# Idle transposes ahead of a kernel's first products, two pool groups in one PSUM tile, and a tail whose order is written out by hand

## The chip, the core and the metric

The kernel runs on one core of a Trainium2 chip. The metric is the device time of one launch in microseconds (us), lower is better. The runs of the kernel before shown here are three, with a median of 2133.31 us (2133.0 to 2134.68); one further execution was profiled, and every view below is of that one.

## What is computed

One layer of a streaming encoder on 256 tokens of width 2048, all in float32. Cut to what matters:

```python
x = x + 0.5 * swiglu(rms_norm(x, ffn1_norm), w_gate, w_up, w_down)        # first FFN, 5632 wide
h = rms_norm(x, mix_norm)
u, q, k, v, g, a_lr = jnp.split(h @ w_in, IN_SPLITS, axis=-1)
y_pool = pool_mixer(u, pool_w, pool_scale)     # 4 groups of 256 channels: trailing mean minus token, @ pool_w[g], * scale
y_gla  = gla_mixer(q, k, v, g, a_lr, ...)      # 4 heads of gated linear attention in chunks of 64, per-head norm, gate
x = x + concat(y_pool, y_gla) @ w_out
x = x + mem_cross_attention(rms_norm(x, xattn_norm), rms_norm(mem, mem_norm), w_q, w_kv, w_o)
x = x + 0.5 * swiglu(rms_norm(x, ffn2_norm), w_gate, w_up, w_down)        # second FFN
return rms_norm(x, final_norm)
```

Weights come from memory once, as float32. Nearly all the work is matrix products of 256 tokens with weights.

## The kernel before, in words

**Split products.** Each float32 operand is written as a rounded high part and a remainder, both of type fp32r: a product is then three matmuls, (high, high), (high, low) and (low, high). Weights arrive in `raw` tiles of 128x2048; ACT casts them to `wh` (line 228) and DVE subtracts to get `wl` (line 229). `in_turn` keeps these splits in their order on each of the two engines. Activations are split the same way into `xs` and `ys`: `split_scaled` does the high part on ACT (line 210) and the remainder on DVE (line 211).

**The stream.** Class `Stream` holds a list of items: units (a load of 1 MB of weights, with the matmuls that use it) and operations between them. `st.op(f, n)` places f behind the n-th unit that follows. `emit` walks the list, splits weights up to two units ahead (one ahead for the first four units) and loads three units ahead, on the queue of SP. So the code has an order, but the order of instructions on each engine is made by the planner (`schedule_with_timeline_sim=True`, line 1291): it runs through the program in a simulated time of its own and places what is ready. Two calls bind it: `issue_after(ins)` keeps instructions behind `ins` on that engine, and `keep_in_program_order` keeps one behind all that stands before it in the code on its engine. Once made, the order is fixed: an engine that waits for one instruction holds all behind it.

**PSUM.** All of PSUM is one pool of four tiles, each 128x2x512 float32 (`ptile`; a half of 512 columns is a bank). A tile is free again when its last reader is done.

**Start (lines 531 to 585, 719 to 724).** `gain_columns` clears a 128x128 tile on DVE and then loads the first norm's 16 rows of weights into it on the queue of ACT; `turn_gains` (539, 540) transposes it on TensorE and copies the columns to `gains`. `x_chunk(c)` transposes the c-th 256 columns of x by four transposes (line 575) and splits them scaled by `gains`; unit c of the first block reads what chunk c makes. Chunk c stands ahead of unit c-1. `x_squares` makes the sums for the norm on ACT (line 244). x chunks and the first weights are loaded in turn on the queue of SP.

**Feed-forward.** `block_t` is an ordinary block: eight units of 24 matmuls of 128x512. `block_s` uses Strassen-like sums for the unit pairs 0, 2 and 4: `part_sums` (lines 346 to 356, through `pair_sums`) makes sums of activations on DVE in a tile `T`, `add_weights` (363 to 367) sums of weights in the same one-buffer tile `T`, and `seven` (401) does seven products.

**Mixer.** `pool_unit` (line 805) does the per-group maps of the pool: for each of four groups g a PSUM tile of its own, with 256 columns of each bank used; `pool_out` scales and splits the result (210, 211) into `ys`. It stands between the block of k, whose evictions use line 266, and the blocks of v. For each GLA head, `scores` makes the scaled copies of q on ACT and DVE (line 933), the score matmuls (941) and the copies to the single tile `ST` (947); `attend` multiplies with v (954, 957) and evicts (963, 965); `head_squares`, `head_norms` (976; 186 reads its PSUM tile) and `head_scale` (207, 990) do the per-head norm. Heads 0 and 1 follow the first block of v, heads 2 and 3 the second; in both, scores stand 1 + i units behind their block, attend 2 + i. Then the two gate blocks (line 292, evicted through lines 265, 266 and 268) follow.

**Tail (lines 1157 to 1231).** The last product is split in token halves h: for each column block nb (four of 512) and half, `end_evict` adds to x on DVE (1188), squares and sums on ACT (1191), and multiplies by the final norm's weights on GpSimd (1193; all but the last block of the second half). `row_factor(h)` makes the factor per token (1196, 186 to 198) and `finish` scales a block (ACT 1207, DVE 1209, or 1203 with both factors) and stores it from the queue of SP (1210): four stores of 256 KB per half. Nothing fixes the order of DVE and ACT here but the planner.

Of the kernel before, what the change touches and what calls it, by code (L numbers as in the profile page):

```python
# [20 lines left out]
NB = 512  # L21
# [4 lines left out]
EPS = 1e-6  # L26
# [4 lines left out]
G_FFN1, G_MIX, G_X, G_MEM, G_FFN2, G_PS, G_HN, G_BA, G_END = 0, 16, 32, 48, 64, 80, 88, 96, 100  # L31
# [61 lines left out]
def build(ctx, tc, I, out):  # L93
    nc = tc.nc
# [22 lines left out]
    def ptile(name):  # L117
        return psum.tile([P, 2, NB], F32, tag="ps", name=name)
# [6 lines left out]
    def uid(s):  # L125
        cnt[0] += 1
        return f"{s}{cnt[0]}"
# [45 lines left out]
    def gcol(i):  # L173
        return gains[:, i : i + 1]
# [3 lines left out]

    def f32(ap):
        return ap.bitcast(F32)  # L180


    def rsqrt(dst, sums, n, w):
# [25 lines left out]
    def split_scaled(dst, kt, src, scale):  # L209
        hi = nc.scalar.activation(dst[:, kt, 0, :], src, AF.Copy, scale=scale)  # L210
        nc.vector.scalar_tensor_tensor(  # L211
            out=dst[:, kt, 1, :], in0=src, scalar=scale, in1=f32(dst[:, kt, 0, :]),
            op0=ALU.mult, op1=ALU.subtract,
        )
        return hi
# [314 lines left out]

    def gain_columns(names, queue):
        t = rows["gain"] = scope["pool"].tile([P, P], F32, tag="gain", name=uid("gain"), bufs=2)
        nc.vector.memset(t, 0.0)
        for name, at, n in names:
            queue.dma_start(t[at : at + n, :], I[name].rearrange("o (k p) -> (o k) p", p=P))

    def turn_gains(lo, hi):
        ps = ptile(uid("pgain"))
        nc.tensor.transpose(ps[:, 0, :P], rows["gain"], ident)
        nc.vector.tensor_copy(gains[:, lo:hi], ps[:, 0, lo:hi])  # L540

    xrows = {}

# [21 lines left out]
    def x_cols(c, n):  # L565

        b = c // (2 * NB)
        return xrows[b][:, :, c - b * 2 * NB : c - b * 2 * NB + n]

    def x_chunk(c):  # L570
        v = ptile(uid("px"))[:, 0, :].rearrange("p (a b) -> p a b", a=2)
        k = 2 * c
        for j in range(2):
            for h in range(2):
                nc.tensor.transpose(  # L575
                    v[:, j, h * P : (h + 1) * P], x_cols((k + j) * P, P)[:, h], ident
                )
        for j in range(2):
            rows["hi", c] = split_scaled(xs, k + j, v[:, j, :], gcol(G_FFN1 + k + j))
# [64 lines left out]

    PAIRS = (0, 2, 4)

    def pair_sums(g, delay):
        def f():
            if g == PAIRS[0]:
# [12 lines left out]
    def ffn(wg, wu, wd, down):  # L662
# [33 lines left out]
        for lo, n in FF_PARTS:  # L696
# [19 lines left out]
                st.op(lambda n=n: turn(gate[0], 4 * (n - 1)), 1)  # L716
            down(wd, 4 * lo, 4 * n, lo + n == FF // NB)

    st.op(lambda: turn_gains(0, G_MIX))
    for c in range(8):  # L720
        st.op(lambda c=c: x_chunk(c), c - 1)
    for c in range(8):
        st.op(lambda c=c: x_squares(c), 6)
    st.op(lambda: finish_norm(8, False), 7)
# [3 lines left out]
    def down_first(wd, k0, nk, last):  # L728
        into_x(wd, ys, 0.5, G_MIX if last else None, k0, nk, src=None if k0 else I["x"][0])

    for g in PAIRS:
        pair_sums(g, 5)
    ffn(I["ffn1_w_gate"][0], I["ffn1_w_up"][0], I["ffn1_w_down"][0], down_first)
    st.op(close_scope, 1)
    st.op(open_scope("s_mix"), 1)
# [62 lines left out]
    def pool_unit(wh, wl):  # L798
        wh, wl = (w.rearrange("p (g t d) -> p g t d", g=4, t=2) for w in (wh, wl))
        for g in range(4):  # L800
            ps = ptile(uid("pp"))
            for dt in range(2):
                parts = [(w, ct, a) for ct in range(2) for w, a in ((wh, 0), (wl, 0), (wh, 1))]
                for n, (w, ct, a) in enumerate(parts):
                    nc.tensor.matmul(
                        ps[:, dt, :S], w[:, g, ct, dt * P : (dt + 1) * P],
                        ys[:, 8 + 2 * g + ct, a, :], start=n == 0, stop=n == 5,
                    )
            mix["pp", g] = ps

    def pool_out(g):
        for dt in range(2):
            split_scaled(ys, 2 * g + dt, mix["pp", g][:, dt, :S], gcol(G_PS + 2 * g + dt))

    def load_a(raw):
        nc.sync.dma_start(
# [189 lines left out]
    for b in range(2):  # L1006
        block_b(wblock(w_in, (4 + b) * NB), xs, ev_v(b))
        for i in range(2):
            h = 2 * b + i
            st.op(lambda h=h: scores(h), 1 + i)  # L1010
            st.op(lambda h=h: attend(h), 2 + i)
            st.op(lambda h=h: head_squares(h), 2 + i)
        st.op(lambda b=b: head_norms(b), 4)
        st.op(lambda b=b: head_scale(b), 5)
    block_a(wblock(w_in, 6 * NB), xs, ev_g(0))
# [137 lines left out]
    def down_end(wd, k0, nk):  # L1153

        acc_ps, kept = {}, []

        def mm(b, k, h, wh, wl):

            wh, wl = (w.rearrange("p (k j n) -> p k j n", j=2, n=NB) for w in (wh, wl))
            for j in range(2):  # L1160
                nb = 2 * b + j
                if nb not in acc_ps:
                    acc_ps[nb] = ptile(uid("pe"))
                for kk in range(2):
                    products(acc_ps[nb][:, h, :], ys, k + kk, h, wh[:, kk, j], wl[:, kk, j],
                             k + kk == 0, k + kk == nk - 1)
                if k == nk - 2:
                    end_evict(nb, h)
# [12 lines left out]

        def end_evict(nb, h):
            cols = slice(nb * NB, (nb + 1) * NB)
# [3 lines left out]
            xn, o = x_cols(nb * NB, NB)[:, h], fin[nb][:, h]  # L1187
            nc.vector.scalar_tensor_tensor(
                out=xn, in0=acc_ps[nb][:, h, :], scalar=0.5, in1=xn, op0=ALU.mult, op1=ALU.add
            )  # L1190
            nc.scalar.activation(o, xn, AF.Square, accum_out=ss[:, h, nb : nb + 1])
            if nb < 3 or h == 0:
                nc.gpsimd.tensor_tensor(out=o, in0=xn, in1=fin["gB"][:, cols], op=ALU.mult)

        def row_factor(h):
            nc.vector.tensor_reduce(out=sums[:, h : h + 1], in_=ss[:, h, :4], axis=AX.X, op=ALU.add)
            rsqrt(Rcol[:, h : h + 1], sums[:, h : h + 1], D, 1)

        def finish(h, c, engine=None):
            cols = slice(c * NB, (c + 1) * NB)  # L1200
            x, o, r = fin[c][:, h], x_cols(c * NB, NB)[:, h], Rcol[:, h : h + 1]
            if h == 1 and c == 3:
                nc.vector.scalar_tensor_tensor(
                    out=o, in0=o, scalar=r, in1=fin["gB"][:, cols], op0=ALU.mult, op1=ALU.mult
                )
            elif engine is nc.scalar:
                nc.scalar.activation(o, x, AF.Copy, scale=r)
            else:
                nc.vector.tensor_scalar_mul(o, x, r)
            nc.sync.dma_start(out[0, h * P : (h + 1) * P, cols], o)  # L1210
# [12 lines left out]

        def ready_sqrt():
            tc.keep_in_program_order(nc.scalar.activation(sums, Rcol, AF.Sqrt))

        st.op(ready_sqrt, 8)
        st.op(last_gain, 2)
        for b in range(2):
            st.op(lambda b=b: fetch_x(b), 1 + 2 * b)  # L1230
        for b in range(2):
            for i, src in enumerate(wwide(wd, b * 2 * NB, k0, nk - 2)):
                st.unit(src, unit(b, 2 * i))
        for b in range(2):
            st.unit(wwide(wd, b * 2 * NB, k0 + nk - 2, 2)[0], end_unit(b))
        st.op(second_half)
# [73 lines left out]
```

## Time and profile before

| what | value |
|---|---|
| median of 3 runs | 2133.31 us |
| the profiled execution's own time | 2133.11 us |
| its span, first to last instruction | 2131.2 us |
| TensorE (PE) busy | 2111.3 us, 99% |
| weight loads (PEld) busy | 1768.5 us, 83% |
| DVE busy | 1427.7 us, 67% |
| ACT busy | 1008.0 us, 47% |
| DMA | 435.91 MB, mean 205 GB/s |

Times in the views count from the span's start. In a row of the timeline the first number is the start, the second how long the row lasts; "x4" says that it merges four instructions, and the bracket gives the engine's idle time before it and what ended that. Matmuls are pipelined: one row's length reaches into the next, so the distance from one start to the next is what a matmul costs. 1.9 us of the profiled execution's own time lie outside its span.

### The profile page before, as it was taken

To read this page: it belongs to the slowest core of one execution; us is meant where nothing else is said; L and a number is where in the kernel's file an instruction comes from. 1 tells how busy PE (TensorE), PEld (TensorE's weight loads), DVE (VectorE), ACT (ScalarE), POOL (GpSimd) and SP (SyncE) were. 2 spreads that over 40 slices of the span, in tenths; PEclk is the share of its full clock that TensorE was granted. 3 is DMA by queue.
4 is the path that set the end of the run, shared out by engine and by line. 5 is a ranking of instruction groups with operands and counts; after the bars stand their busy time and mean duration, and the time that the engine had idled before them with its cause. 6 is when DMAs were issued, how large, how long until landed. Compare 5 with 4: busy or idle time off the path is not lost.

```text
span 2131.2 us, 24070 instructions
## 1 busy us (share of the span) xinstructions
PE 2111.3 (99%) x10032; PEld 1768.5 (83%) x10032; DVE 1427.7 (67%) x1189; ACT 1008.0 (47%) x890; POOL 14.2 (1%) x41
## 2 busy tenths in 40 slices
PE   9999999999999999999999999999999999999998
PEld 7878888888888888888888888888888888888886
DVE  8876588856864576565666454567874888658744
ACT  7554354534534545455445443445443455434433
POOL 0000000000000000000000000000000000000001
PEclk9999999999999999999999999999999999999999
DMA  7556665566656655557654555666576665766663
GB/s 277 197 189 234 224 221 195 186 233 226 227 178 234 221 162 180 167 185 278 222 190 161 167 169 171 195 207 207 175 247 217 214 209 175 249 212 223 221 217 119
DMA packets 143316, 435.91 MB, mean 205 GB/s; under 512 B 9828, under 2 KB 13000, under 8 KB 142824
## 3 DMA queue, kind: packets, MB, share of 16 engines
q1 hardware_dynamic: 143176, 434.38, 60.5%
q8 instruction: 78, 1.28, 0.2%
q14 instruction: 30, 0.25, 0.0%
q10 hardware_dynamic: 32, 0.01, 0.0%
HBM read 417.58 MB, written 16.78 MB: 204 GB/s over the span
## 4 chain that ended last, share of the span: by engine, by line
PE 98%; DVE 1%; issue 0%; ACT 0%; DMA 0%; SPq 0%; DVEq 0%; ACTq 0%
PE pt L307 58%; PE pa L292 15%; PE pt L401 12%; PE pb L307 6%; PE pe L307 3%; PE ph L691 1%; PE pl L1084 1%; PE pv L1119 1%; PE px L621 0%; DVE wl L229 0%; ACT wh L228 0%; DMA x<-in_x 0%; PE px L575 0%; PE po L954 0%; PE pa L832 0%
## 5 line engine op out<-in xcount | busy, mean ns | idle before, releaser
L229 DVE TENSOR_TENSOR wl<-raw,wh 128x2048 fp32r<-128x2048 f32 (+2 forms) x328 | 740.2, 2258 | 544.5 <-ACT wh L228 543.9
L228 ACT CAST wh<-raw 128x2048 fp32r<-128x2048 f32 (+2 forms) x328 | 618.5, 1886 | 721.7 <-PE pt L307 490.5
L307 PE MATMUL pt<-wh,xs 128*128 128x512 f32 x1952 | 618.6, 390 | 0.0
L307 PE MATMUL pt<-wh,ys 128*128 128x512 f32 x1728 | 534.7, 389 | 0.0
L307 PEld LDWEIGHTS pt<-wh,xs 128*128 128x128 f32 x1952 | 366.6, 188 | 75.7
L307 PE MATMUL pt<-wl,xs 128*128 128x512 f32 x976 | 380.8, 390 | 0.0
L307 PEld LDWEIGHTS pt<-wh,ys 128*128 128x128 f32 x1728 | 324.1, 188 | 67.0
L307 PE MATMUL pt<-wl,ys 128*128 128x512 f32 x864 | 336.3, 389 | 0.0
L292 PE MATMUL pa<-xs,wh 128*128 128x512 f32 x896 | 317.1, 398 | 2.1 <-DVE t L266 1.7
L292 PE MATMUL pa<-xs,wl 128*128 128x256 f32 x896 | 248.8, 281 | 0.0
L307 PEld LDWEIGHTS pt<-wl,xs 128*128 128x128 f32 x976 | 183.5, 188 | 37.9
L292 PEld LDWEIGHTS pa<-xs,wh 128*128 128x128 f32 x896 | 167.7, 188 | 41.2 <-issue 2.0
L307 PEld LDWEIGHTS pt<-wl,ys 128*128 128x128 f32 x864 | 162.2, 188 | 33.5
L292 PEld LDWEIGHTS pa<-xs,wl 128*128 128x128 f32 x896 | 169.2, 189 | 1.6 <-issue 0.2
L228 ACT CAST wh<-T 128x2048 fp32r<-128x2048 f32 x54 | 103.3, 1912 | 135.6 <-DVE T L367 93.3
L229 DVE TENSOR_TENSOR wl<-T,wh 128x2048 fp32r<-128x2048 f32 x54 | 123.6, 2288 | 65.3 <-ACT wh L228 65.3
L307 PE MATMUL pb<-wh,xs 128*128 128x512 f32 x384 | 121.7, 392 | 0.5 <-DVE ys L211 0.5
L401 PE MATMUL pt<-wh,xe 128*128 128x512 f32 x324 | 108.7, 389 | 0.0
L229 DVE TENSOR_TENSOR xl<-raw,xh 128x1536 fp32r<-128x1536 f32 x54 | 94.5, 1750 | 2.7 <-ACT xh L228 2.7
L228 ACT CAST xh<-raw 128x1536 fp32r<-128x1536 f32 x54 | 79.9, 1479 | 28.9 <-PE pt L401 28.8
L307 PEld LDWEIGHTS pb<-wh,xs 128*128 128x128 f32 x384 | 72.0, 188 | 15.6 <-DVE ys L211 0.7
L401 PE MATMUL pt<-xh,xs 128*128 128x512 f32 x216 | 78.6, 389 | 1.7 <-DVE sg L452 1.7
(203 smaller groups left out, 1666.3 us busy)
## 6 DMA issues: line engine op xcount, KB each, us to landing
raw<-in_ffn_w_down SPq DMA_DIRECT2D x88, 1024.0 KB, 5.5
raw<-in_ffn_w_up SPq DMA_DIRECT2D x80, 1024.0 KB, 5.0
raw<-in_ffn_w_gate SPq DMA_DIRECT2D x77, 1024.0 KB, 5.0
raw<-in_w_in SPq DMA_DIRECT2D x32, 1024.0 KB, 5.2
raw<-in_xattn_w_kv SPq DMA_DIRECT2D x32, 1024.0 KB, 5.2
raw<-in_w_out SPq DMA_DIRECT2D x16, 1024.0 KB, 6.2
raw<-in_xattn_w_q SPq DMA_DIRECT2D x16, 1024.0 KB, 5.2
raw<-in_xattn_w_o SPq DMA_DIRECT2D x16, 1024.0 KB, 5.6
```

What stands on the lines that cost most here:

```text
L228: in_turn("scalar", lambda: nc.scalar.copy(hi, src))
L229: in_turn("vector", lambda: nc.vector.tensor_tensor(out=lo, in0=src, in1=f32(hi), op=ALU.subtract))
L292: nc.tensor.matmul(o, w, x, start=k == 0 and i == 0, stop=last and i == 1)
L307: nc.tensor.matmul(ps, a, w, start=first and i == 0, stop=last and i == 2)
L401: nc.tensor.matmul(banks[n], x, w, start=first and j == 0, stop=not later and n in ("P1", "P5", "P6", "P7") and j == 2,)
L691: nc.tensor.transpose(v[:, i, h * P : (h + 1) * P], g[:, h, i * P : (i + 1) * P], ident)
L1084: nc.tensor.matmul(ps[:, t, :M], ys[:, 4 * h + d, a, tok], xa["K"][:, d, b, :], start=i == 0, stop=i == 11,)
L1119: nc.tensor.matmul(ps[:, d, :S], xa["V"][:, m, a, col], xa["PT"][:, m, b, :], start=i == 0, stop=i == 5,)
```

## The change

1. **Start.** Twelve transposes of the identity matrix into a PSUM tile that nobody reads are placed ahead of everything on TensorE. The gain tile of the first norm is no longer cleared, only its 16 rows are transposed, and the first weight splits on DVE queue behind the copy of the gains. Chunks 3 to 7 of x stand one unit earlier.
2. **Pair sums of the first FFN** stand behind unit 4, 5 and 6 instead of all behind unit 5, and on DVE they queue behind the latest weight split.
3. **Pool.** Two groups share a PSUM tile, a bank each; both halves of a group lie in one bank.
4. **Heads 2 and 3** stand one unit earlier.
5. **Tail.** All product halves stand ahead of the first row factor; every step of DVE and ACT is kept in the order of the code; the blocks of the second half with nb = 2 and 3 take both factors on DVE and skip GpSimd; the blocks (0, 1) and (0, 3) are finished and stored in two halves each; there are ten stores instead of eight, all still on the queue of SP.

```diff
+    def spare_transposes(n):
+        ps = ptile(uid("pwarm"))
+        for _ in range(n):
+            nc.tensor.transpose(ps[:, 0, :P], ident, ident)
...
     def gain_columns(names, queue):
-        nc.vector.memset(t, 0.0)
+        if len(names) > 1:
+            nc.vector.memset(t, 0.0)
...
     def turn_gains(lo, hi):
-        nc.tensor.transpose(ps[:, 0, :P], rows["gain"], ident)
-        nc.vector.tensor_copy(gains[:, lo:hi], ps[:, 0, lo:hi])
+        n = hi if lo == 0 else P
+        nc.tensor.transpose(ps[:, 0, :n], rows["gain"][:n, :], ident[:n, :n])
+        copied = nc.vector.tensor_copy(gains[:, lo:hi], ps[:, 0, lo:hi])
+        if lo == 0:
+            latest["vector"] = copied
...
     def pair_sums(g, delay, behind=False):
+            if behind:
+                with tc.issue_after(latest["vector"].ins):
+                    sums_of(g)
...
+    st.op(lambda: spare_transposes(12))
     st.op(lambda: turn_gains(0, G_MIX))
-    for c in range(8):
-        st.op(lambda c=c: x_chunk(c), c - 1)
+    st.op(lambda: x_chunk(0))
+    for c in range(1, 8):
+        st.op(lambda c=c: x_chunk(c), c - 1 if c < 3 else c - 2)
...
-    for g in PAIRS:
-        pair_sums(g, 5)
+    for n, g in enumerate(PAIRS):
+        pair_sums(g, 4 + n, behind=True)
...
         for g in range(4):
-            ps = ptile(uid("pp"))
+            if g % 2 == 0:
+                two = ptile(uid("pp"))
+            ps = two[:, g % 2, :].rearrange("p (a b) -> p a b", a=2)
...
-            st.op(lambda h=h: scores(h), 1 + i)
-            st.op(lambda h=h: attend(h), 2 + i)
-            st.op(lambda h=h: head_squares(h), 2 + i)
+            at = 1 + i - b
+            st.op(lambda h=h: scores(h), at)
+            st.op(lambda h=h: attend(h), at + 1)
+            st.op(lambda h=h: head_squares(h), at + 1)
...
         def second_half():
-            row_factor(0)
-            finish(0, 0, nc.scalar)
-            finish(0, 3)
-            mm(0, nk - 2, 1, *kept[0])
-            finish(0, 1, nc.scalar)
-            finish(0, 2)
-            mm(1, nk - 2, 1, *kept[1])
-            row_factor(1)
-            for c in range(4):
-                finish(1, c, nc.scalar if c == 1 else None)
+            act, dve, half = nc.scalar, nc.vector, NB // 2
+            for b in range(2):
+                mm(b, nk - 2, 1, *kept[b])
+            row_factor(0, lambda: in_order(update(0, 1)))
+            in_order(square(0, 1))
+            weigh(0, 1)
+            finish(act, 0, 0)
+            in_order(update(1, 1))
+            in_order(square(1, 1))
+            weigh(1, 1)
+            finish(act, 0, 1, 0, half)
+            in_order(update(2, 1))
+            in_order(square(2, 1))
+            in_order(update(3, 1))
+            in_order(square(3, 1))
+            finish(dve, 0, 2)
+            finish(dve, 0, 3, 0, half)
+            finish(act, 0, 1, half, NB)
+            row_factor(1)
+            finish(dve, 1, 2)
+            finish(act, 1, 0)
+            finish(dve, 1, 3)
+            finish(act, 1, 1)
+            finish(dve, 0, 3, half, NB)
```

`update`, `square` and `weigh` are the three steps of the old `end_evict`. `row_factor` now issues its five steps itself, each kept in order, and puts the first update of the second half between its square root on ACT and its first reciprocal on DVE.

More of the change, by code (lines that the diff above doesn't have):

```diff
@@ L645, in build, with pair_sums, sums_of @@
     PAIRS = (0, 2, 4)
-    def pair_sums(g, delay):
+    def pair_sums(g, delay, behind=False):
         def f():
+            if behind:
+                with tc.issue_after(latest["vector"].ins):
+                    sums_of(g)
+            else:
+                sums_of(g)
+        def sums_of(g):
             if g == PAIRS[0]:
@@ L805, in pool_unit @@
                     nc.tensor.matmul(
-                        ps[:, dt, :S], w[:, g, ct, dt * P : (dt + 1) * P],
+                        ps[:, dt, :], w[:, g, ct, dt * P : (dt + 1) * P],
                         ys[:, 8 + 2 * g + ct, a, :], start=n == 0, stop=n == 5,
@@ L812, in pool_out @@
         for dt in range(2):
-            split_scaled(ys, 2 * g + dt, mix["pp", g][:, dt, :S], gcol(G_PS + 2 * g + dt))
+            split_scaled(ys, 2 * g + dt, mix["pp", g][:, dt, :], gcol(G_PS + 2 * g + dt))
     def load_a(raw):
@@ L1166, in mm @@
                              k + kk == 0, k + kk == nk - 1)
-                if k == nk - 2:
-                    end_evict(nb, h)
+                if k == nk - 2 and h == 0:
+                    update(nb, h)
+                    square(nb, h)
+                    weigh(nb, h)
         def unit(b, k):
@@ L1180, in end_unit, with update @@
             return fn
-        def end_evict(nb, h):
-            cols = slice(nb * NB, (nb + 1) * NB)
+        def update(nb, h):
             if h == 0:
@@ L1186, in end_evict @@
                 fin[nb] = t[:, : 2 * NB].rearrange("p (h n) -> p h n", h=2)
-            xn, o = x_cols(nb * NB, NB)[:, h], fin[nb][:, h]
-            nc.vector.scalar_tensor_tensor(
+            xn = x_cols(nb * NB, NB)[:, h]
+            return nc.vector.scalar_tensor_tensor(
                 out=xn, in0=acc_ps[nb][:, h, :], scalar=0.5, in1=xn, op0=ALU.mult, op1=ALU.add
             )
-            nc.scalar.activation(o, xn, AF.Square, accum_out=ss[:, h, nb : nb + 1])
-            if nb < 3 or h == 0:
-                nc.gpsimd.tensor_tensor(out=o, in0=xn, in1=fin["gB"][:, cols], op=ALU.mult)
@@ L1195, in row_factor, with square @@
[L1195 to L1207, printed above, removed]
-            else:
-                nc.vector.tensor_scalar_mul(o, x, r)
-            nc.sync.dma_start(out[0, h * P : (h + 1) * P, cols], o)
+        def square(nb, h):
+            return nc.scalar.activation(
+                fin[nb][:, h], x_cols(nb * NB, NB)[:, h], AF.Square, accum_out=ss[:, h, nb : nb + 1]
+            )
@@ new lines, in weigh, with in_order, row_factor @@
+        def weigh(nb, h):
+            nc.gpsimd.tensor_tensor(
+                out=fin[nb][:, h], in0=x_cols(nb * NB, NB)[:, h],
+                in1=fin["gB"][:, nb * NB : (nb + 1) * NB], op=ALU.mult,
+            )
+        def in_order(ins):
+            return tc.keep_in_program_order(ins)
+        def row_factor(h, between=None):
+            t, r = sums[:, h : h + 1], Rcol[:, h : h + 1]
+            v, q = chain[:, 0, h : h + 1], chain[:, 1, h : h + 1]
+            in_order(nc.vector.tensor_reduce(out=t, in_=ss[:, h, :4], axis=AX.X, op=ALU.add))
+            in_order(nc.vector.tensor_scalar(
+                out=v, in0=t, scalar1=0.25 / D, scalar2=0.25 * EPS, op0=ALU.mult, op1=ALU.add
+            ))
+            in_order(nc.scalar.activation(q, v, AF.Sqrt))
+            if between:
+                between()
+            in_order(nc.vector.reciprocal(out=r, in_=q))
+            in_order(nc.vector.tensor_scalar(
+                out=v, in0=v, scalar1=r, scalar2=q, op0=ALU.mult, op1=ALU.add
+            ))
+            in_order(nc.vector.reciprocal(out=r, in_=v))
@@ new lines, in finish @@
+        def finish(engine, h, c, lo=0, hi=NB, queue=nc.sync):
+            at = slice(c * NB + lo, c * NB + hi)
+            x, r = fin[c][:, h, lo:hi], Rcol[:, h : h + 1]
+            o = x_cols(c * NB, NB)[:, h, lo:hi]
+            if engine is nc.scalar:
+                in_order(nc.scalar.activation(o, x, AF.Copy, scale=r))
+            elif h == 1 and c >= 2:
+                in_order(nc.vector.scalar_tensor_tensor(
+                    out=o, in0=o, scalar=r, in1=fin["gB"][:, at], op0=ALU.mult, op1=ALU.mult
+                ))
+            else:
+                in_order(nc.vector.tensor_scalar_mul(o, x, r))
+            queue.dma_start(out[0, h * P : (h + 1) * P, at], o)
```

## The prediction

> **What bounds the kernel.** I read the page's head first, then the chain that ended last, then whom TensorE waited for.
>
> ```profile
> PE 2111.3 (99%) x10032; PEld 1768.5 (83%) x10032; DVE 1427.7 (67%) x1189; ACT 1008.0 (47%) x890; POOL 14.2 (1%) x41
> ...
> PE 98%; DVE 1%; issue 0%; ACT 0%; DMA 0%; SPq 0%; DVEq 0%; ACTq 0%
> ```
>
> ```profile
> PE pgain L539 <- DMA gain<-in_ffn_norm: 4.1, 1, 4.1
> PE pt L401 <- DVE sg L452: 1.7, 1, 1.7
> PE pa L292 <- DVE t L266: 1.7, 1, 1.7
> PE po L954 <- DVE ST L947: 1.0, 1, 1.0
> PE pp L805 <- DVE k L266: 0.6, 1, 0.6
> PE pb L307 <- DVE ys L211: 0.5, 1, 0.5
> ```
>
> TensorE is busy for 99% of the span and 98% of the chain lies on it. No matmul of the products is taken away, so only what it stands still, what it runs slowly, and what comes behind its last matmul can change: the 4.1 us at the start, single waits of 0.5 to 1.7 us, and the tail. The second row (first FFN) is in no part that the change touches. The profiled execution took 2133.1 us, of which 1.9 lie outside the span; I sum against that, and it stands 0.2 below the shown median of 2133.3.
>
> **Start.** The timeline of TensorE, from its second group of transposes on:
>
> ```profile
> 5.76 1.12 PE L575 MATMUL px<-ident,x 128*128 128x128 f32 x4 [0.34 <-DMA x<-in_x]
> 6.53 0.78 PE L307 MATMUL pt<-wh,xs 128*128 128x512 f32 x1
> 7.11 0.63 PE L307 MATMUL pt<-wl,xs 128*128 128x512 f32 x1
> 7.53 1.05 PE L307 MATMUL pt<-wh,xs 128*128 128x512 f32 x2
> 8.39 0.58 PE L307 MATMUL pt<-wl,xs 128*128 128x512 f32 x1
> 8.80 0.62 PE L307 MATMUL pt<-wh,xs 128*128 128x512 f32 x2
> 9.27 0.40 PE L307 MATMUL pt<-wl,xs 128*128 128x512 f32 x1
> ```
>
> ```profile
> 6.50:7.20 0.70, 0.70 (x4) 0.60 (x3) 0.00 (x0) 0.52 (x1) 0.00 (x0) 1.00 1.02 353
> ```
>
> From 7.53 to 8.39 are two products, 0.43 each; from 8.80 to 9.27 two, 0.235 each. The clock doubles at about 8.8, though the column of the granted clock in the second fence (third number from the end) reads 1.00 already: in this stretch the distances of the starts decide. The five products from 6.53 to 8.80 took 2.27; at 0.235 they take 1.18, so 1.09 were lost. The four transposes ahead took 0.77 (5.76 to 6.53), and those of chunk 4 (16.82 to 17.18, next fence) 0.36:
>
> ```profile
> 12.70 1.22 DVE L229 TENSOR_TENSOR wl<-raw,wh 128x1024 fp32r<-128x1024 f32 x1 [0.35 <-ACT wh L228]
> ...
> 14.54 0.40 PE L307 MATMUL pt<-wl,xs 128*128 128x512 f32 x1
> ...
> 16.82 0.60 PE L575 MATMUL px<-ident,x 128*128 128x128 f32 x4
> 17.18 0.71 PE L307 MATMUL pt<-wh,xs 128*128 128x512 f32 x2
> ```
>
> That is 0.41 more, so the slow clock costs at most 1.5. The change lets TensorE work from the moment the identity is there:
>
> ```profile
> 1.07 0.29 POOL masks.py:199 TENSOR_SCALAR_AFFINE_SELECT ident<-ident 128x128 f32<-128x128 f32 x1
> ```
>
> That is 1.4, 2.7 before its first matmul now, which waits for the gains until 4.1. Twelve transposes at the 0.19 of the slow ones (0.77 / 4) make 2.3 and end by then, so they delay nothing. If activity is what raises the clock, it took from 4.1 to 8.8, 4.7 us with a hole; begun at 1.4 it comes by about 6.1, before the first product.
>
> Does TensorE get the gain? The first products can't come before x chunk 1, whose DMA ended the wait at 5.76, and this load is not moved; so the earlier gain load (no memset ahead of it) is hidden behind it and brings nothing; nor does the order of the gains' copy and the first split on DVE, which hold it already. The next supply is tight: the low parts of unit 1 are done at 13.92 (12.70 + 1.22), and TensorE first uses them at 14.54. That leaves 0.62. Chunks 3 to 7 stand a unit earlier, so chunk 4's transposes (16.82) can move into that hole, another 0.36. The cap is 0.98, and I take **0.9**; the ends are 0 (clock not sooner) and 1.5 (supply sooner too).
>
> [...]
>
> **Pair sums.** DVE's three groups are moved behind weight splits, to where DVE has less room:
>
> ```profile
> 45.00:65.00 20.00, 20.00 (x90) 16.53 (x90) 16.13 (x12) 12.54 (x11) 0.00 (x0) 1.00 0.57 204
> ```
>
> DVE's busy time is the third: 3.9 of 20 us are free in this stretch, while a group of sums takes under 3 (six short passes on at most 512 columns, against 1.22 for the 1024 columns of the row at 12.70: an estimate of 2.3 to 2.8). One group surely comes here, a second perhaps in part. I take 0; ends -0.5 (a split comes late) and +0.2. If that cover is gone, the late one is the weight split of the first seven-product units.
>
> **Pool.** The waits' list has two here, 0.6 for L266 and 0.5 for L211: the fourth group waits for a PSUM tile of the k block, the v block for one of the pool's own. TensorE around the second:
>
> ```profile
> 829.02 0.28 PE L805 MATMUL pp<-ys,wl 128*128 128x256 f32 x1
> 829.14 0.28 PE L805 MATMUL pp<-ys,wh 128*128 128x256 f32 x1
> 829.89 0.50 PE L307 MATMUL pb<-wh,xs 128*128 128x512 f32 x1 [0.47 <-DVE ys L211]
> ```
>
> Starts lie 0.12 apart, so the one at 829.89 is 0.63 late, 0.16 more than the idle time says, as each row's length reaches into the next. The same on the other's 0.6 makes 0.8. With two tiles for four groups, both are there when the pool starts, since the k block holds only two of four, and the v block gets one of the k block's. Nothing else is late behind it: **1.4**, ends 0 and 1.4.
>
> Against it stands that a group's two halves now share a bank.
>
> ```profile
> ACT xs L210 <- DVE xs L211: 26.6, 24, 2.4
> ```
>
> Where x chunks share a bank so, ACT waited for DVE 24 times, 1.1 us each on the mean. The pool has four such pairs, so ACT could be 4 us later with its next weight cast; units there last 5.5 us and splits run two ahead, so it stays beside TensorE.
>
> **Heads 2 and 3.** The other two waits of the list stand at the end of the first gate block: the attend (954) for the copies to `ST`, 1.0, and the next block's first product for L266, 1.7. With 0.16 each they cost 1.2 and 1.8, 3.0 in all. The first is a bare chain of head 3 (scores, copies, attend) with no product left to put between; the second is four PSUM tiles full: two of the block, head 3's and the norm's. How head 3 got so late:
>
> ```profile
> 894.13 1.05 PE L207 MATMUL ps<-diag,ones 128*128 128x128 f32 x8
> 895.12 0.65 PE L941 MATMUL pq<-m,k 128*64 128x256 f32 x4
> ```
>
> Head 2's scores came only at 895.12, right behind the head scaling, which takes a PSUM tile ahead of them in the code, and head 3 follows head 2. With scores(2) ahead of the gate block, head 3's chain falls among the block's products and its tile is back when the next block begins. I take **2.5**, not 3.0, because L266 can still be queued behind a weight split of 2.3 us. Ends: 3.0, and -6 (the slower rival below).
>
> **Tail.**
>
> ```profile
> 2120.95 1.53 DVE L1209 TENSOR_SCALAR x<-O,Rcol 128x512 f32<-128x512 f32 x2
> 2122.40 0.68 DVE L1188 SCALAR_TENSOR_TENSOR x<-pe,x 128x512 f32<-128x512 f32 x1
> 2123.87 0.16 DVE L1196 TENSOR_REDUCE sums<-ss 128x1 f32<-128x4 f32 x1 [0.79 <-ACT O L1191]
> ...
> 2125.05 0.16 DVE L198 RECIPROCAL Rcol<-chain 128x1 f32<-128x1 f32 x1
> ...
> 2126.12 0.74 DVE L1203 SCALAR_TENSOR_TENSOR x<-x,Rcol,gB 128x512 f32<-128x512 f32 x1
> ```
>
> ```profile
> 2121.10 6.54 SPq L1210 DMA_DIRECT2D out<-x  x8
> ```
>
> ```profile
> 2121.28 0.39 PE L307 MATMUL pe<-wh,ys 128*128 128x512 f32 x1
> ```
>
> The last product is there at about 2121.7, but its update on DVE runs at 2122.40, behind two scalings: 0.7 lost. From there the square takes till 2123.87 and the row factor till 2125.21 (2125.05 + 0.16), 1.34 more. In the new order the update comes ahead of the scalings: 2121.7 + 0.68 + 0.79 + 1.34 = 2124.5. ACT has a half finish between its last square and the second square root (about 0.4), beside which two of DVE's steps (0.3) run, so 2124.6, 0.6 sooner. The first block then takes 0.74 (the form of the last row) where it took about 0.45, so it goes out 0.4 to 0.5 sooner. Behind that the stores bind: SP's row ends at 2127.64 (2121.10 + 6.54), 0.8 after DVE. Four and a half blocks go out instead of four; at the 353 GB/s of the window above, half a block of 256 KB is 0.37. GpSimd's work gets less and lies beside. **0.1**; ends -0.3 (the two further stores hold SP) and 0.7.
>
> **Sum.** 0.9 + 0 + 1.4 + 2.5 + 0.1 = 4.9; 2133.1 - 4.9 = 2128.2, and 0.2 more for the shown median: **2128.4**.
>
> **Rivals.**
> - The clock comes no sooner (that part doesn't do what it says): 2128.4 + 0.9 = 2129.3. For it: the wait for x chunk 1 leaves a hole in the activity, as before. Against: activity starts 2.7 us sooner.
> - The gate block still waits: head 3's norm keeps its place, and if L266 stands behind the weight split again, the 1.8 stay: 2130.2. With the first rival too: 2131.1.
> - Slower than before: head 2's scores now take a PSUM tile ahead of the gate block, whose second tile must then wait for a release:
>
> ```profile
> 879.00:887.00 8.00, 8.00 (x48) 7.03 (x46) 1.00 0.43 146
> ```
>
> ```profile
> 888.55 0.16 DVE L186 TENSOR_SCALAR chain<-pn 128x4 f32<-128x4 f32 x1
> ```
>
> The first row is the gate block's own line: 24 pairs of matmuls in 8 us, 0.33 each. With its first tile alone TensorE has eight of a unit's sixteen pairs, 2.7 us. It starts with head 2's scores ahead of it, some 0.8 later than this window (an estimate), and runs dry at about 882.5. If the next tile to come back is the norm's, read at 888.55 to 888.7, TensorE stands 6.2: 2134.6. It decides from 4.9. Against it: head 1's tile or head 2's own is enough too, and head 2's needs only its copies (under 1.4 us), for which DVE can be free.
>
> **How the numbers follow.** About 0.2%, 4.3 us, is what a measurement of this kernel can tell from no change, so faster means below 2129.0. Chances: forecast 0.52 (2127.1 to 2129.4), clock no sooner 0.17, gate block waits 0.20, both 0.05, slower by the PSUM tile 0.06. Faster: 0.8 of the first, 0.4 of the second, 0.2 of the third, 0.53 together; slower by over 4.3 only if the last goes beyond 2137.6, 0.03; the rest, 0.44, is within. The range 2126.6 to 2131.3 takes in all but the last case and the edges.
>
> **What would show it.** Starts 0.235 apart from the first product on; no wait at L805 or the first L307 of v; none at the last L954 and at the gate block's first L292; L1188 of the last block at about 2121.7 less what came before. Wrong: starts of 0.43 behind x chunk 1, a new wait at the first gate block's second tile, or a wait in the first FFN's seven products behind a weight split.

## The result, and the profile after

| | median us | executions | ratio to the kernel before |
|---|---|---|---|
| before | 2133.31 | 7, 2132.7 to 2134.95 | |
| changed | 2140.46 | 7, 2137.93 to 2142.16 | 1.0031 [1.0021, 1.0041] |

The changed kernel is 7.1 us slower; the prediction had 2128.4, 4.9 faster. The profiled execution of it took 2142.16 us with a span of 2140.3, 9.1 more than before's 2131.2; it is 1.7 above the median, so the places below add up to more than 7.1. One execution of a later kernel (e10) took 4451.9 us, over twice the others, for a reason not known, and its ratio leaves that one out. All line numbers of the changed kernel are higher by 6 to 50 (first products 313 instead of 307, seven products 407, gate blocks 298, head scaling 213, pair sums and weight sums 352 to 373).

The page's head, TensorE's share of the chain, and whom TensorE waited for:

```profile
PE 2120.1 (99%) x10044; PEld 1774.1 (83%) x10044; DVE 1427.7 (67%) x1188; ACT 1008.0 (47%) x892; POOL 14.0 (1%) x40
...
PE 96%; DVE 2%; issue 1%; ACT 1%; DMA 0%; SPq 0%; DVEq 0%; ACTq 0%
```

```profile
PE pa L298 <- DVE t L272: 2.6, 1, 2.6
PE pt L407 <- DVE sg L458: 1.5, 1, 1.5
PE pwarm L186 <- POOL ident masks.py:199: 1.4, 1, 1.4
PE pt L407 <- DVE xl L235: 1.3, 1, 1.3
PE pt L313 <- ACT wh L234: 0.8, 1, 0.8
PE pt L313 <- ACT xs L216: 0.7, 1, 0.7
PE pt L407 <- ACT wh L234: 0.6, 1, 0.6
PE po L975 <- DVE ST L968: 0.6, 1, 0.6
```

The two waits of the pool (L805 and the one of the v block's first product, in the list of before) are gone; three new ones of 0.6 to 1.3 are there in the first FFN and one of 0.7 ahead of the first product, and the gate block's is 2.6 instead of 1.7. How far the same matmul lies behind its place of before tells where each us went:

| place | before | after | behind |
|---|---|---|---|
| first product | 6.53 | 7.75 | 1.2 |
| first FFN, unit 3 | 26.30 | 28.73 | 2.4 |
| first FFN, seven products | 99.45 | 101.96 | 2.5 |
| the same, next block | 149.15 | 157.78 | 8.6 |
| end of the first FFN's last block | 700.07 | 708.70 | 8.6 |
| first v block | 830.23 | 836.86 | 6.6 |
| second gate block | 922.10 | 930.92 | 8.8 |
| last product | 2121.28 | 2130.18 | 8.9 |
| end of the span | 2131.2 | 2140.3 | 9.1 |

So: start +2.5, first FFN +6.1, pool -2.0, heads +2.2, tail +0.15. Between these places next to nothing is lost.

**Start.** The row of before, then the timeline of the changed kernel:

```profile
5.47 0.47 ACT L210 ACTIVATE xs<-px,gains 128x256 fp32r<-128x256 f32 x1 [0.16 <-PE px L575]
```

```profile
5.94 1.11 PE L585 MATMUL px<-ident,x 128*128 128x128 f32 x4 [0.44 <-DMA x<-in_x]
...
6.71 0.62 ACT L234 CAST wh<-raw 128x512 fp32r<-128x512 f32 x1 [1.30 <-DMA raw<-in_ffn_w_gate]
7.23 0.83 ACT L216 ACTIVATE xs<-px,gains 128x256 fp32r<-128x256 f32 x2
...
7.75 0.80 PE L313 MATMUL pt<-wh,xs 128*128 128x512 f32 x1 [0.70 <-ACT xs L216]
...
10.91 1.48 PE L313 MATMUL pt<-wh,xs 128*128 128x512 f32 x3
```

x chunk 1 landed at 5.94, nearly as before, but chunk 0's scaling on ACT now stands behind the second weight cast, which waits for its load until 6.71. The products then start 0.43 apart until 13.5; before, only until 8.8. How much this costs differs from one profiled execution to the next: at unit 3 of the first FFN, e2, e3 and e6 below, which keep the transposes and this order, lie -0.2, 3.2 and 2.3 behind the kernel before, and the changed kernel 2.4.

**First FFN.** Two stretches of the changed kernel's timeline:

```profile
109.47 1.91 ACT L234 CAST wh<-T 128x2048 fp32r<-128x2048 f32 x1 [11.61 <-DVE T L373]
...
111.42 0.73 PE L407 MATMUL pt<-wh,xe 128*128 128x512 f32 x2 [0.60 <-ACT wh L234]
...
113.22 0.49 PE L313 MATMUL pt<-wh,xs 128*128 128x512 f32 x1 [0.83 <-ACT wh L234]
```

```profile
147.66 0.50 PE L407 MATMUL pt<-xl,xs 128*128 128x512 f32 x1 [1.29 <-DVE xl L235]
...
149.93 0.67 PE L407 MATMUL pt<-wh,xe 128*128 128x512 f32 x1 [1.54 <-DVE sg L458]
...
150.82 1.05 PE L407 MATMUL pt<-wh,xe 128*128 128x512 f32 x2
```

ACT sat idle for 11.6 us until the sums in `T` were there; then TensorE ran out of split weights. In the kernel before, the planner had put the three groups of pair sums on DVE between 8.7 and 30.0, ahead of the first weight sum at 37.46; in the changed kernel they lie between 31.7 and 61.9, and the first weight sum begins at 47.95. At 147 to 150 two holes come close together, and behind them the products lie 0.43 apart again. The view by stretches gives the granted clock (third number from the end) there:

```profile
146.69:150.10 3.41, 0.90 (x3) 0.47 (x4) 3.41 (x4) 0.19 (x1) 0.00 (x0) 1.00 0.85 282
150.10:153.51 3.41, 3.41 (x9) 2.65 (x10) 3.33 (x4) 1.14 (x2) 0.00 (x0) 0.50 0.07 28
153.51:156.92 3.41, 3.41 (x17) 2.80 (x16) 1.41 (x1) 3.35 (x2) 0.00 (x0) 1.00 0.67 205
914.69:918.10 3.41, 0.79 (x6) 0.70 (x6) 3.38 (x4) 2.00 (x3) 0.00 (x0) 1.00 0.20 32
918.10:921.51 3.41, 3.41 (x12) 2.92 (x12) 3.32 (x8) 1.51 (x3) 0.00 (x0) 0.50 0.77 286
```

Two stretches of 3.41 us each have a granted clock of 0.50, each right behind one in which TensorE was busy for 0.9 and 0.8 of 3.41. In the first stretch, nine products at 0.43 instead of 0.23 cost 1.8. The profile of before has no such stretch: its granted clock reads 1.00 from 8.9 to 2121.

**Heads.**

```profile
885.49 0.65 PE L962 MATMUL pq<-m,k 128*64 128x256 f32 x4
...
902.75 1.05 PE L213 MATMUL ps<-diag,ones 128*128 128x128 f32 x8
903.64 0.60 PE L975 MATMUL po<-ST,v 128*128 128x256 f32 x2
...
911.20 0.65 PE L962 MATMUL pq<-m,k 128*64 128x256 f32 x4
...
913.05 0.67 PE L975 MATMUL po<-ST,v 128*128 128x256 f32 x2 [0.57 <-DVE ST L968]
...
917.62 0.47 PE L298 MATMUL pa<-xs,wh 128*128 128x512 f32 x1 [2.62 <-DVE t L272]
```

Head 2's scores come 9.6 sooner than before (885.49 against 895.12). Its attend doesn't: at 903.64 it follows the head scaling (902.75), as it did at 900.64 before. So head 3 (911.20, before 904.82) still stands at the block's end, with both waits. In the second of them the eviction (L272) runs on DVE at 916.78, right behind a weight split of 2.29 that began at 914.45; before, it was likewise (909.48, behind the split at 907.15).

**Pool and tail.** The pool's last product and the v block's first now follow each other 0.12 apart. On SP, ten stores:

```profile
836.50 0.28 PE L826 MATMUL pp<-ys,wh 128*128 128x256 f32 x1
836.62 0.40 PE L313 MATMUL pb<-wh,xs 128*128 128x512 f32 x1
```

```profile
2129.01 7.60 SPq L1260 DMA_DIRECT2D out<-x  x10
...
2130.18 0.39 PE L313 MATMUL pe<-wh,ys 128*128 128x512 f32 x1
...
2133.20 0.16 DVE L1244 RECIPROCAL Rcol<-chain 128x1 f32<-128x1 f32 x1
```

The last row factor is there 3.2 behind the start of the last product (2133.36 - 2130.18); before it was 3.9 (2125.21 - 2121.28). The end of the span is 10.1 behind it, before 10.0.

### The profile page after: what moved, and what is told of

Its sections match the earlier page's. It is cut to its first block, busy times and chain, and to the rows that moved or that the text cites. A ratio compares the mean times of both kernels' runs of the same rounds, so it can differ in the third digit from the quotient of the medians.

```text
span 2140.3 us, 24091 instructions
## 1 busy us (share of the span) xinstructions
PE 2120.1 (99%) x10044; PEld 1774.1 (83%) x10044; DVE 1427.7 (67%) x1188; ACT 1008.0 (47%) x892; POOL 14.0 (1%) x40
## 4 chain that ended last, share of the span: by engine, by line
PE 96%; DVE 2%; issue 1%; ACT 1%; DMA 0%; SPq 0%; DVEq 0%; ACTq 0%
PE pt L313 57%; PE pa L298 15%; PE pt L407 11%; PE pb L313 6%; PE pe L313 3%; PE ph L708 1%; DVE wl L235 1%; PE pl L1106 1%; PE pv L1141 1%; PE px L631 0%; ACT wh L234 0%; DVE xl L235 0%; PE pp L826 0%; DVE T L369 0%; DMA raw<-in_ffn_w_gate 0%
```

## Experiments

The kernel before ran beside all of them, at medians of 2134.18 (e1 to e4), 2134.32 (e5 to e8) and 2133.46 (e9 to e12); its means there lie closer together, between 2133.9 and 2134.1. Every ratio is to the kernel before of the same session, and each experiment has one profiled execution. First the changed kernel with one part undone, and one part alone.

### e1: without the idle transposes

```diff
-    st.op(lambda: spare_transposes(12))
```

> The changed kernel without its 12 idle transposes. Theory: it is these that put the second weight cast ahead of chunk 0's scaling on ACT (the planner takes TensorE for late), so that the first product came at 7.75 instead of 6.53 and the clock rose at 13.6 instead of 8.8. Without them the first product is back at 6.5 and TensorE is 2.5 us sooner by 20 us. If all of it reaches the end: 2140.5 - 2.5 = 2138.0. Rival: in the first FFN TensorE waits for DVE and ACT at 110 to 148 anyway; then it arrives there sooner and stands longer, and the end stays at 2140.5.

Measured: 2139.07, ratio 1.0023 [1.0014, 1.0032]. ACT and TensorE of it:

```profile
5.32 0.47 ACT L210 ACTIVATE xs<-px,gains 128x256 fp32r<-128x256 f32 x1
...
6.43 0.78 PE L307 MATMUL pt<-wh,xs 128*128 128x512 f32 x1
...
6.57 0.62 ACT L228 CAST wh<-raw 128x512 fp32r<-128x512 f32 x1 [0.79 <-DMA raw<-in_ffn_w_gate]
```

The order on ACT is back and the first product comes at 6.43. All four waits at 108 to 122 are there in their old sizes (974, 1230, 530 and 512 ns from start to start), only 2.4 sooner. So the rival falls: what the start gains reaches the end. The median gained 1.4, not 2.5; the mean gained 2.0 (2140.65 to 2138.70), and the 2.5 was one execution's. That the planner reorders ACT because it takes TensorE for late is a reading; the run shows only that the order comes and goes with the transposes. The two waits at 143.66 and 146.09 have another shape here, 2.10 and 0.80 instead of 1.68 and 1.94, and no half clock follows them (the mean granted clock is 0.998, the changed kernel's 0.997), so the profiled execution gains more than the start: its span is 2135.7.

### e2: pair sums at their old place

```diff
-        pair_sums(g, 4 + n, behind=True)
+        pair_sums(g, 5)
```

> The changed kernel with the pair sums where they were. Theory: the sums, moved to behind the weight splits, cost DVE its lead; the waits of the seven-product units at 110 to 124 (2.4 us in four) and the two at 146 to 148 (3.2, for one of 1.9 before) go, and with the two the half clock of 3.4 us behind them (1.7): 2140.5 - 5.4 = 2135.1. Rival: the lead was lost in the first 30 us, by the order on ACT there; the waits stay, and so does 2140.5.

Measured: 2134.08, ratio 1.0005 [0.9996, 1.0014]: 6.4 less than the changed kernel. The first FFN has the one wait of 2.09 (at 138.93) that it had before, and no half clock (mean granted clock 0.998). The pair sums are most of the loss. In the spans (2131.7 against 2140.3) 6.1 of the 8.6 lie in the first FFN and most of the rest in the start, where the products are 0.34 apart and less from 7.70 on, not 0.43 until 13.5. The executions spread more than the others, from 2133.46 to 2138.2. A second finding stands in its start:

```profile
4.17 0.28 PE L547 MATMUL pgain<-ident,gain 16*128 16x16 f32 x1
4.56 1.11 PE L585 MATMUL px<-ident,x 128*128 128x128 f32 x4
5.92 0.66 PE L585 MATMUL px<-ident,x 128*128 128x128 f32 x4 [0.24 <-DMA x<-in_x]
7.70 0.50 PE L313 MATMUL pt<-wh,xs 128*128 128x512 f32 x1 [1.13 <-ACT xs L216]
8.04 0.39 PE L313 MATMUL pt<-wl,xs 128*128 128x512 f32 x1
```

Four transposes take 1.11 at 4.56 and 0.66 at 5.92, and the first products are at once 0.23 to 0.34 apart: the clock had risen by 5.92, before any product had run.

### e5: pair sums moved, alone

```diff
-    for g in PAIRS:
-        pair_sums(g, 5)
+    for n, g in enumerate(PAIRS):
+        pair_sums(g, 4 + n, behind=True)
```

(`pair_sums` takes `behind` as in the change)

> The kernel before with the pair sums moved, and nothing else. Theory: the move alone takes DVE's lead over TensorE; the waits of 0.3 to 1.0 us at about 108 to 122 and the longer ones at 139 to 146 are there again, 4 to 6 us together: 2134.2 + 5 = 2139.2 (2134.2 is the kernel before in the runs just made). Rival: the loss needs the later start of the first products and their order on ACT too: then 2134.2, with the one wait of 1.9 at 139.

Measured: 2136.92, ratio 1.0014 [1.0005, 1.0023], 2.6 more than before. The waits are those of e1, and TensorE stands 2.9 longer than before between 107 and 147, but no stretch falls to half clock (mean granted clock 0.998). The mechanism was right; alone it costs half of what was expected.

### e6: the sums in a tile of their own

```diff
-        t = scope["pool"].tile([P, 4 * NB], F32, tag="T", name=uid("T"))
+        t = scope["pool"].tile([P, 2 * NB], F32, tag="S", name=uid("S"))
```

> The changed kernel, the pair sums at their new place but in an SBUF tile of their own instead of T. Theory: the loss is T, of which there is one: sums and weight sums take turns on it, so that the first weight sum can begin only when the second pair sum is through (47.95 instead of 37.46). With a tile apart the weight sums lead again, the waits at 110 to 148 go: 2140.5 - 5 = 2135.5. Rival: it is DVE's time, about 2.5 us for each group, in a stretch where it has none to spare; then the waits stay, about 2140.5.

Measured: 2138.78, ratio 1.0022 [1.0013, 1.0031]. Both theories hold in part. The weight sums begin at 39.80 and the four waits at 110 to 124 are gone, so those came from the one tile `T`. The two at 143 to 147 stay, with the half clock (mean granted clock 0.997; the row at 147.26 lasts 0.79):

```profile
144.99 0.50 PE L407 MATMUL pt<-xl,xs 128*128 128x512 f32 x1 [1.29 <-DVE xl L235]
...
147.26 0.79 PE L407 MATMUL pt<-wh,xe 128*128 128x512 f32 x1 [1.54 <-DVE sg L458]
```

Both end with work of DVE, which fits the rival: it is DVE's time. The kernel before shows that there is little to make up with; DVE is the third busy time of the row:

```profile
80.00:100.00 20.00, 20.00 (x90) 16.57 (x89) 19.31 (x18) 9.88 (x6) 0.00 (x0) 1.00 0.65 217
```

### e3: heads at their old place

```diff
-            at = 1 + i - b
-            st.op(lambda h=h: scores(h), at)
+            st.op(lambda h=h: scores(h), 1 + i)
```

(attend and squares likewise, at 2 + i)

> The changed kernel with the heads' steps where they were. Theory: scores of head 2 ahead of the gate block only put eight copies on DVE ahead of head 1's sum of squares, so the norm, the scaling, the attend of head 2 behind it and head 3 all come later; the wait at the end of the gate block grew from 1.9 to 2.9 us and the clock fell to half for 3.4 us. Undone: the two waits are 1.3 and 1.9 as before, no half clock, 2140.5 - 2.3 = 2138.2. [...]

Measured: 2140.87, ratio 1.0033 [1.002, 1.0045]; no gain. The waits are 1.3 and 1.9 from start to start, as expected, but the half clock came all the same (918.7 to 922.1; mean granted clock 0.997, as in the changed kernel). The theory that the heads' part made the half clock falls; the part is about neutral. The same two waits stand in the kernel before (idle times of 1.0 and 1.7) without a half clock: the granted clock reads 1.00 from 900 to 925 there. So their length alone doesn't decide; what does isn't shown.

### e7: heads 2 and 3 ahead of the first scaling

On the kernel before, with the pool's and the heads' parts:

```diff
-        st.op(lambda b=b: head_norms(b), 4)
-        st.op(lambda b=b: head_scale(b), 5)
+        st.op(lambda b=b: head_norms(b), 6 - 2 * b)
+        st.op(lambda b=b: head_scale(b), 7 - 2 * b)
```

> The kernel before with the pool's and the heads' part, and the norm and scaling of heads 0 and 1 two units later, so that they stand behind the attend of head 2 and the scores of head 3. Theory: the early scores brought nothing because attend 2 and scores 3 stood behind that scaling in the order of PSUM tiles; now both waits at the end of the gate block (1.1 and 1.7 us) go: 2132.3 (pool alone) - 2.8 = 2129.5. Rival: the gate block's eviction then waits for the scaling and holds its two PSUM tiles, so that the next block waits as long: 2132.3.

Measured: 2128.63 (2128.19 to 2129.2), ratio 0.9975 [0.9965, 0.9985]. TensorE in it:

```profile
892.30 0.65 PE L943 MATMUL pq<-m,k 128*64 128x256 f32 x4
...
898.92 0.59 PE L956 MATMUL po<-ST,v 128*128 128x256 f32 x2
...
900.58 1.05 PE L207 MATMUL ps<-diag,ones 128*128 128x128 f32 x8
...
905.87 0.47 PE L292 MATMUL pa<-xs,wh 128*128 128x512 f32 x1
```

Head 3's scores (892.30) and attend (898.92) stand inside the gate block, the scaling (900.58) behind them, and the next block begins at 905.87 with no wait. Heads 2 and 3 are worth 3.7 on top of the pool, once the scaling is out of their way; between the spans of e4 and e7 (2129.2 and 2126.3) it is 2.9, the size of the two waits. The theory holds. No run moved the scaling with heads 2 and 3 left at their old place, so whether their earlier place is needed at all stays open.

### e4: the pool alone

```diff
-            ps = ptile(uid("pp"))
+            if g % 2 == 0:
+                two = ptile(uid("pp"))
+            ps = two[:, g % 2, :].rearrange("p (a b) -> p a b", a=2)
```

> The kernel before with the change of the pool groups alone. Theory: the two waits at the pool go, 1.4 us: 2133.3 - 1.4 = 2131.9, and the products there follow each other without a gap. Rival: two halves in one PSUM bank make ACT wait for DVE, the next weight cast is late and TensorE waits for it instead: 2133.3 or more.

Measured: 2132.29, ratio 0.9992 [0.9983, 1.0001]: 1.9 less than before, which the interval alone doesn't tell from nothing; but the span is 2.0 shorter too (2129.2), and no start at the pool is late. ACT does wait for DVE there, twice 2.0 us (0.5 before), as the prediction feared, and TensorE doesn't notice:

```profile
ACT ys L210 <- DVE ys L211: 4.0, 2, 2.0
```

### e8 and e11: idle transposes with the order of ACT held

e8 is the kernel before with the 12 transposes; the weight casts of unit 0 are kept behind the scalings that stood ahead of them:

```diff
             split_weights(hi[:, part], lo[:, part], raw[:, part])
+            if u == 0 and c < 3 * NB:
+                latest["scalar"] = rows[(("hi", 0, 0), ("hi", 1, 0), ("hi", 1, 1))[c // NB]]
```

> The kernel before with the 12 idle transposes alone, and ACT's first casts and scalings held in an order with chunk 0's first scaling ahead of the second weight cast. [...]

Measured: 2134.18, ratio 0.9999 [0.999, 1.0008]. The first product comes at 6.73 and the next 0.59 behind it (7.32), as in the kernel before (0.58), so the clock had not risen ahead of the products here; in e2 it had. What makes the difference isn't shown.

e11 is e7 with the same hold, the change's edits of the gains and, beside the 12, three more transposes (its sums of squares for chunk 0 stand behind chunk 1's scalings):

```diff
     st.op(lambda: x_chunk(0))
+    st.op(lambda: spare_transposes(3))
     for c in range(1, 8):
```

> The kernel with the heads apart, with 12 idle transposes ahead of the gains and 3 more between the first two x chunks, the gain load as changed, and the first casts and scalings on ACT and DVE held in the order that lets the first product start at 6.5. [...]

Measured: 2132.73, ratio 0.9993 [0.9984, 1.0002], 4.1 above e7. In the start the clock came early:

```profile
5.29 0.85 PE L186 MATMUL pwarm<-ident 128*128 128x128 f32 x3
6.14 1.08 PE L585 MATMUL px<-ident,x 128*128 128x128 f32 x4
6.88 0.65 PE L313 MATMUL pt<-wh,xs 128*128 128x512 f32 x1
7.37 0.40 PE L313 MATMUL pt<-wl,xs 128*128 128x512 f32 x1
7.61 0.62 PE L313 MATMUL pt<-wh,xs 128*128 128x512 f32 x2
```

The second product follows after 0.49, the next after 0.24: full speed from 7.37 on, where before it came at 8.8. But new waits stand at 13.8 (0.8) and 58.2 (2.2, for ACT), the second with a half clock behind it (mean granted clock 0.998, e7's 0.999). The planner's order is another one far beyond the start, and that costs more than the clock brings. Which edit does it isn't shown: e8 has the 12 transposes and the hold, e12 below the gains' edits, and neither has these waits, which leaves the three further transposes, the squares of chunk 0, or the edits together.

### e9, e10, e12: the tail and the rest of the start, on e7

e9 adds the whole of the change's `second_half` to e7:

```diff
+            row_factor(0, lambda: in_order(update(0, 1)))
...
+            finish(dve, 0, 3, half, NB)
```

> The kernel of the run before with the heads apart (2128.6), with the change's tail added. Theory: the last row factor comes 0.7 sooner, but four and a half blocks go out behind it instead of four, so the last landing is where it was, 8.6 us behind the start of the last product: 2128.6, within 0.2. Rival: what hid the gain in the changed kernel was that profile's own; the factor's 0.7 reaches the end: 2127.9.

Measured: 2128.72, ratio 0.9975 [0.9964, 0.9986]: as expected, nothing. The last store is landed 8.6 behind the start of the last product, as in the changed kernel.

e10 stores the block whole ahead of the factor:

```diff
-            finish(dve, 0, 3, 0, half)
+            finish(dve, 0, 3)
...
-            finish(dve, 0, 3, half, NB)
```

> The same, with the last block of the first 128 rows scaled and stored whole ahead of the second row factor instead of its second half behind everything. Theory: four blocks go out behind the factor, 0.68 apart, and the half block's 0.47 at the end goes; DVE needs some 0.1 more ahead of the factor: 2128.6 - 0.35 = 2128.2, the last landing 8.2 to 8.3 behind the start of the last product. Rival: the stores ahead of the factor are still on their way and push the four back: 2128.6.

Measured: 2127.82, ratio 0.9969 [0.9956, 0.9982], 0.9 less than e9. Its stores on SP, nine:

```profile
2115.27 7.00 SPq L1241 DMA_DIRECT2D out<-x  x9
```

SP's wait for the last store ends 8.1 behind the start of the last product instead of 8.6, so the trace shows 0.5 of the 0.9. It is the fastest version of the study.

e12 adds the gains' and the chunks' edits to e7, without transposes (`turn_gains` also as in the change):

```diff
-        nc.vector.memset(t, 0.0)
+        if len(names) > 1:
+            nc.vector.memset(t, 0.0)
...
-        st.op(lambda c=c: x_chunk(c), c - 1)
+        st.op(lambda c=c: x_chunk(c), c - 1 if c < 3 else c - 2)
```

> The kernel with the heads apart, with the start's other edits but no idle transposes: the gains' tile not cleared, their copy ahead of the first weight split, chunks 3 to 7 a unit sooner. Theory: the load of x chunk 1 bounds the first product, so the gains bring nothing, and chunk 4 comes 0.4 sooner into a hole that is there only while DVE is late: 2128.6 to 2128.2. Rival: the earlier chunks stand ahead of weight splits on ACT and DVE and cost lead: 2130 or more, with a longer wait at 139.

Measured: 2128.91, ratio 0.9974 [0.9964, 0.9985]: nothing, as expected.

## Why the prediction was wrong, point by point

- **Start, 0.9 forecast, 2.5 lost in the profiled execution.** The step that failed is "twelve transposes ... delay nothing". On TensorE that holds (the gains' transpose ran at 4.17). What came late was chunk 0's scaling on ACT, by the planner's order: without the transposes the order is back (e1). The working took for granted that the scaling of before (5.47) stays ahead of the second cast. The clock step was right in that it can rise on transposes alone (e2: 1.11 for four at 4.56, 0.66 at 5.92), but not in its size: it took the 4.7 us of the kernel before, from the first activity on and with a hole in it, for enough. In the profiled changed kernel, with its first transpose at 1.4, the products still lay 0.43 apart until 13.5, while in e2, with the same order, they lay 0.34 and less apart from 7.70 on. What decides between the two isn't shown.
- **Pair sums, 0 forecast, 2.6 lost alone and 6.4 in the whole.** The step that failed is reading 3.9 free us in 45 to 65 as cover. A free stretch is no cover when the engine is full behind it: DVE is busy for 19.3 of 20 at 80 to 100, and the lead that the sums took was not made up before TensorE ran dry at 110 and 146, far from the edit. The prediction did name the sign, a wait in the seven products behind a weight split, but priced it at 0.5. Nor did it see that sums and weight sums share the one tile `T`, although the code says so; e6 shows that the four first waits come from that. In the whole change's profile a stretch of 3.41 us at a granted clock of 0.50 (from 150.10, 1.8 lost) stands right behind the second pair of holes, in e5's none does; that the two differ by this alone isn't shown.
- **Pool, 1.4 forecast.** Right: 2.0 in the spans, 1.9 in the medians ([-0.2, 3.6] by the interval), no wait left, and ACT's waits on the shared bank (twice 2.0 us, e4) were beside TensorE.
- **Heads, 2.5 forecast, about nothing won.** The step that failed: "With scores(2) ahead of the gate block, head 3's chain falls among the block's products". Scores were not what held head 3; attend 2 and scores 3 stood behind the head scaling in both kernels. The prediction named that scaling ("takes a PSUM tile ahead of them in the code"), and the change moved only one of the three steps past it. e7 takes it out of the way, and the two waits, put at 3.0, go (2.9 in the spans, 3.7 in the medians).
- **Tail, 0.1 forecast.** Right in its steps: the factor came 0.7 sooner (forecast 0.6), and the four and a half blocks behind it ate it up; the half block is 0.5 (forecast 0.37; e10).
- **Rivals.** The gate block still waited, as the second rival said, with the eviction behind a weight split as it named. The slower one, by the second gate tile, didn't come: no wait there. The clock that comes no sooner had its condition come true in the profiled execution (0.43 apart until 13.5), but not at its price of 0.9. None of the rivals had the planner's order or DVE's lead, and so the range ended at 2131.3.

## What to carry to other kernels

Where a planner makes each engine's order, an instruction that costs nothing on its own engine can still reorder the others: look at the order of the engines beside it, not only at the idle time it fills. Work moved later on an engine that feeds TensorE spends lead, and is paid where that engine is next full, so read the whole stretch until the lead would be back. And before moving a step forward, find what stands right ahead of its successor: scores moved 9.6 us and gained nothing until the scaling was moved too.

## What the runs showed of the hardware

- In the changed kernel the granted clock was 0.50 for 3.41 us twice, from 150.10 and from 918.10, and 1.00 right before and behind. TensorE was busy for 0.90 and 0.79 of the 3.41 us ahead. In the first stretch products of 512 columns lay 0.43 apart, against 0.23 in a full stream, so the holes ahead of it came with 1.8 more than their own length.
- The two holes of the gate block (1.3 and 1.9 from start to start) had no half clock behind them in the kernel before (1.00 from 900 to 925) and had one in e3 (918.7 to 922.1).
- In the start, products of 512 columns lay 0.43 apart until 8.8 in the kernel before and until 13.5 in the changed kernel. In e2, which like the changed kernel has the idle transposes, four transposes took 1.11 at 4.56 and 0.66 at 5.92, and the products were 0.34 apart and less from the first one on.
- In e7, without the holes of the gate block, eight executions lie within 1.0 us; thirty of the kernel before in the same session spread over 3.3. The mean granted clock was 0.998 or 0.999 in e7's, and 0.997 to 0.999 in the others. That the clock makes the difference fits, but isn't shown, as one execution of each was profiled.
